# Per-partition scaling of attention probabilities as 64 instructions on ScalarE or VectorE, in a two-layer decoder kernel

## The chip, the cores and the metric

The kernel runs on one core of one Trainium2 chip. The metric is the device time of one execution in microseconds (us). Before the change the median of three runs is 612.57 us (611.25 to 612.8).

The engines are named as the profile names them: PE is TensorE (matmuls), PEld its weight load, DVE is VectorE, ACT is ScalarE, POOL is GpSimd, and SP is the queue that issues the loads of weights. Each engine works through its own queue in order and waits on semaphores for the others.

## The reference

Two layers over 256 positions of width 1024. Layer 0 mixes positions with a recurrent block, layer 1 with sparse attention; a squared-ReLU MLP of width 4096 follows each, and all sit between RMS norms. The change is in the attention of layer 1, 16 heads of width 64 in 4 groups of keys and values. It has three branches; with 256 positions, all of the 4 key blocks may be selected and the window of 512 holds everything, so two branches are dense causal attention over their own keys and values, and the third attends to 15 compressed keys:

```python
p = jnp.where(mask, jnp.exp(s - m), 0.0)
return p / jnp.maximum(jnp.sum(p, axis=-1, keepdims=True), 1e-30)
...
o = g[..., 0:1] * o_c + g[..., 1:2] * o_s + g[..., 2:3] * o_w
```

For each query row and each of the two dense branches the probabilities are thus divided by their sum and multiplied by a sigmoid gate: one factor per row and branch.

## The kernel before

Every fp32 product is made of three matmuls on halves: each operand is split into a rounded part (`hi`) and the rest (`lo`), and hi*hi, hi*lo and lo*hi are added (lines 305 to 307). So each weight piece of 128x1024 that is loaded costs a cast on ScalarE or VectorE (`whi`) and a subtraction on VectorE (`wlo`, line 310), beside its load on SP's queue. There are 5 buffers for raw weights and 7 for split ones.

The MLPs are loops written out by hand. The two mixers are sections whose order comes from a planner, `Plan`, that runs when the kernel is built. Each task is added with an engine (or a list of engines, each with a duration and a penalty), what it reads and writes, and a due time. `list_schedule` makes a first plan from the due times and a random shift drawn with a seed; six rounds of `forwards` and `backwards` replan it, each task going to the engine on which its end plus its penalty comes first; the plan that ends first sets the order in which instructions are emitted on each engine. Planner durations and due times set an order only; on the chip each engine waits for what it needs. The seed of the attention section is the second of `SEEDS`.

In the attention section, q, k and v are projected, and the 16 heads follow one another in the order of `heads`. Positions lie on 128 partitions in two query blocks: block 0 sees 128 keys and block 1 sees 256, for each of the two branches (`b`). So a head has four rows of probabilities, in the buffer `pt`: two of 128x128 and two of 128x256. The steps of a head, with the line numbers of the profile:
- `scores`: matmuls of q and k (1062, 1063); line 1069 on VectorE adds the positional term and the mask and leaves in `mx` the extreme of each row; line 1072 on ScalarE takes Exp with `mx` as its bias and accumulates the sum into `sm`.
- `rescale`: lines 1081, 1082 and 1084 on VectorE turn `sm` (128x4, one column per query block and branch) into the factors; line 1090 on VectorE multiplies `pt` by them, both branches of a query block in one instruction, so two instructions a head, of 128x256 and 128x512.
- `transposes`: line 1102 on TensorE turns the probabilities; line 1105 on ScalarE (`pth`) and line 1106 on VectorE (`ptl`) take them out of PSUM in two halves.
- `pv`: for each pair of heads, matmuls with the values (1121, 1132, 1134), then `osum` (1138 on ScalarE, 1141 on VectorE) and its split into `oh` and `ol`.

There are 3 buffers `pt`, 4 of `mx` and `sm`, and 4 transposed ones. Between the heads TensorE has other work of the section: projections of later q and k (809, 821 take them out of PSUM), and the first half of the output projection (487 adds it to `xt`). The second half follows behind the last head, and then the MLP of layer 1. Casts (`sa`, `sb`, `kh`, `oh`, line 313) may go to ScalarE or VectorE, as the planner finds.

Of the kernel before, what the change touches and what calls it, by code (L numbers as in the profile page):

```python
# [15 lines left out]
OP = mybir.AluOpType  # L16
# [3 lines left out]
P = 128  # L20
# [11 lines left out]
NPT, NTH = 3, 4  # L32
TSTAGE, FPS = 4.4, 3.0
CST = (0.5, 4.0, 8.5, 12.0)
SEEDS, ROUNDS, SHIFT = (11, 19), 6, 1.5
HPEN, LPEN, APEN, LEAD = 0.5, 1.0, 0.0, 9.0
WARM = 16
NI, NFINE = 3, 3
SQN = 2
# [37 lines left out]
class Plan:  # L77
# [8 lines left out]
    def add(self, eng, dur, fn=None, r=(), w=(), t=0.0, lag=None):  # L86

        if fn is None:
            eng, fn = eng, dur
        if isinstance(eng, str):  # L90
            eng = [(eng, dur, 0.0)]
        i, deps = len(self.tasks), set()
        for k in r:
            if k in self.writer:
                deps.add(self.writer[k])
            self.readers.setdefault(k, []).append(i)
        for k in w:
            deps.update(self.readers.pop(k, ()))
            if k in self.writer:
                deps.add(self.writer[k])  # L100
            self.writer[k] = i
        deps.discard(i)
        self.tasks.append((eng, fn, sorted(deps), t, lag))
# [113 lines left out]
def trunk_kernel(ctx: ExitStack, tc: tile.TileContext, x_in, vec_in, const_in, w2_in, wts, out):  # L217
    nc = tc.nc
    ctx.enter_context(tc.manual_schedule())
    pe, dve, act, pool = nc.tensor, nc.vector, nc.scalar, nc.gpsimd  # L220
# [9 lines left out]
    def bank(i):  # L230
        return psum.tile([P, 512], F32, name="bank%d" % i, tag="bank%d" % i)
# [258 lines left out]
    with ExitStack() as ph:  # L490
        rg = ph.enter_context(tc.tile_pool(name="rg", bufs=1))
        sec = Section()
        add, table = sec.add, sec.table
# [33 lines left out]
        wz = bank(7)[:, :S]  # L527
        for i in range(WARM):
            pe.matmul(wz, warm[:, :P], warm, start=True, stop=True)

        x2 = rg.tile([P, KC, S], F32, name="x2")
        for k in range(KC):
            g = vec[:, V_GM + k:V_GM + k + 1]
            t = 0.6 * k - 3
            add("act", 0.4, lambda e, k=k, g=g: e.activation(hh[:, k], xt[:, k], AF.Identity, scale=g),
                r=[("xt", k), "vec0"], w=[("hh", k)], t=t)
            add("dve", 0.4, lambda e, k=k, g=g: e.scalar_tensor_tensor(  # L537
                hl[:, k], xt[:, k], g, hh[:, k].bitcast(F32), op0=OP.mult, op1=OP.subtract), r=[("xt", k), "vec0"],
                w=[("hh", k)], t=t)
# [3 lines left out]
        for q in range(4):  # L543
            for i in range(NFINE):
                w = slice(256 * q, 256 * q + 256)
                hi, lo, rw = hi_t[i][:, w], lo_t[i][:, w], raw_t[i][:, w]
                rk = [("raw0", i, q), ("raw", i)]
                t = 1.2 * q + 0.3 * i - 2.9
                add([("dve", 0.2, 0.0), ("act", 0.31, 0.5)], copy(hi, rw), r=rk, w=[("hi0", i, q)], t=t)
                add("dve", 0.34, diff(lo, rw, hi), r=rk + [("hi0", i, q)], w=[("lo0", i, q)],  # L550
                    t=t + 0.1)
        for a, b, n in ((0, 2, 2), (0, 1, 1), (4, 6, 2), (4, 5, 1), (0, 4, 1)):
            add("dve", 0.07 + 0.267 * n, lambda e, a=a, b=b, n=n: e.tensor_tensor(
                x2[:, a:a + n], x2[:, a:a + n], x2[:, b:b + n], op=OP.add), r=[("x2", b + i) for i in range(n)],
                w=[("x2", a + i) for i in range(n)], t=4 + a / 4)
# [44 lines left out]
        def nextbank():  # L600
            zb["n"] += 1
            return (0, 1, 2, 3, 4, 5, 7)[(zb["n"] - 1) % 7]
# [102 lines left out]
        for m in range(8):  # L705
            wh, wl, wk = sec.weight("out", m, to + 2.65 * m)
            b = nextbank()
# [7 lines left out]
            t = to + 2.65 * (m + 1)  # L715
# [55 lines left out]
    with ExitStack() as ph:  # L771
        at = ph.enter_context(tc.tile_pool(name="at", bufs=1))
        sec = Section()
        add, weight, proj_t, zview, table = sec.add, sec.weight, sec.proj, sec.bank, sec.table
# [79 lines left out]
        for i in range(2):  # L854
            pecol = (V_PEK, V_PEV)[i]
            add("pool", 0.15, lambda e, i=i, c=pecol: e.tensor_copy(zfs[i][:, 60], vec[:, c:c + 16]), w=[("zf", i, "p")],
                t=-5)
# [218 lines left out]
        def rescale(s, t):  # L1076
            p, c, hf = heads[s]
            h = (2 * p + hf) * 4 + c
            sm, pt = sms[s % 4], pts[s % NPT]
            k2 = [("sm", s % 4, j) for j in range(4)]  # L1080
            add("dve", 0.07, lambda e: e.tensor_scalar(sm, sm, 1e-30, None, op0=OP.max), w=k2, t=t)
            add("dve", 0.09, lambda e: e.reciprocal(sm, sm), w=k2, t=t)
            s2_ = sm.rearrange("p (q b) -> p q b", q=2)
            add("dve", 0.07, lambda e: e.tensor_tensor(s2_, s2_, gts[:, :, h, 1:3], op=OP.mult),
                r=[("gt", 0), ("gt", 1)], w=k2, t=t)
            for qc in range(2):
                nk = (qc + 1) * P
                v = pt[:, qc * 2 * P:qc * 2 * P + 2 * nk].rearrange("p (b k) -> p b k", b=2)
                add("dve", (0.34, 0.6)[qc],
                    lambda e, v=v, qc=qc, nk=nk: e.tensor_tensor(  # L1090
                        v, v, sm[:, 2 * qc:2 * qc + 2, None].to_broadcast([P, 2, nk]), op=OP.mult),
                    r=[("sm", s % 4, 2 * qc + b) for b in range(2)], w=[("pt", s % NPT, qc, b) for b in range(2)], t=t + 0.2)

        def transposes(s, t):
            pt = pts[s % NPT]
# [51 lines left out]
        def out_t(half, m, b, t, step):  # L1147
            wh, wl, wk = weight("o%d" % half, m // 2, t)
            z = zview(("out", half, m), b, zcols)
            for ks in ((0, 1), (2, 3)) if half == 0 else ((0, 1), (2,), (3,)):  # L1150
                def run(e, ks=ks):
                    for kk in ks:
                        o = (m % 2) * 512 + kk * P
                        k = half * 4 + kk
                        mm3(z(), wh[:, o:o + P], wl[:, o:o + P], oh[k], ol[k], kk == 0, kk == 3)
                add("pe", 0.33 * len(ks), run, r=wk + [(n, half * 4 + kk) for n in ("oh", "ol") for kk in ks],
                    w=[("ps", b)], t=t)
                t += step * len(ks) / 2
            add("dve", 0.34, lambda e: residual(z(), m), r=[("ps", b)], w=[("xt", m)], t=t)
            return t  # L1160
# [29 lines left out]
        for i, (nm, c) in enumerate(fillers):  # L1190
            t = T0 + 4 * i * step
            b = i % 2
# [3 lines left out]
        for m in range(8):  # L1196
            t = T0 + (n0 + 2 * m) * step
            events.append((t, 0, lambda m=m, t=t: out_t(0, m, (len(fillers) + m) % 2, t, step)))
        for s in range(16):
            events.append((T0 + s * T, 1, lambda s=s: scores(s, T0 + s * T)))  # L1200
            events.append((T0 + (s + 1) * T - 1.5, 1, lambda s=s: rescale(s, T0 + (s + 1) * T - 1.5)))
            events.append((T0 + (s + 1.6) * T, 1, lambda s=s: transposes(s, T0 + (s + 1.6) * T)))
# [8 lines left out]
        for m in range(8):  # L1211
            t = out_t(1, m, (2, 3, 4, 0, 1)[m % 5], te - 2 + 1.4 * m, PJ)
# [131 lines left out]
```

## Time and profile before

| | before |
|---|---|
| median of three runs | 612.57 us |
| profiled execution, its time | 611.19 us |
| profiled execution, its span from first to last instruction | 609.1 us |
| PE busy | 580.3 us |
| DVE busy | 455.2 us |
| ACT busy | 362.2 us |
| mean granted TensorE clock | 0.981 |

The span is the time between the first and the last instruction; the time holds 2.1 us more that lie around it. Busy times are unions of the instructions' times. An instruction's duration overlaps with its neighbour's on the same engine by some 0.1 us where neither waits, so that a row of instructions costs less than the sum of their durations; the distance from start to start is then the cost of one.

### The profile page before, as it was taken

Reading aid. Unit: us, or ns where it says so; the run is one execution under the profiler, and the core shown is the slowest. Engines: PE = TensorE matmul, PEld = TensorE weight load, DVE = VectorE, ACT = ScalarE, POOL = GpSimd, SP = SyncE. Lnnn points to the kernel's source line nnn. Section 1 sums busy time; section 2 is a strip of 40 time slices with the busy share of each in tenths; the row PEclk is TensorE's granted clock in tenths of the full one; section 3 lists DMA queues with packets and bytes.
Section 4 is the critical chain, followed back from the end, with each engine's and each line's share of the span. In section 5 each row is a group of like instructions: output and inputs, shape, how many; then the busy total and the mean of one; then the engine's idle time right before and its main releaser. Section 6 shows DMA issues by size and latency. Waiting matters only on the chain.

```text
span 609.1 us, 12332 instructions
## 1 busy us (share of the span) xinstructions
PE 580.3 (95%) x4867; PEld 565.9 (93%) x4867; DVE 455.2 (75%) x929; ACT 362.2 (59%) x692; POOL 47.8 (8%) x57
## 2 busy tenths in 40 slices
PE   8979999999999999999999877899999999999994
PEld 7969999999999999999998766798999999999994
DVE  6999998767666556469989998999876677355432
ACT  7889775856564334256768866676675655343320
POOL 2210000000001122130010000000000000132220
PEclk9989999999999999999999998899999999999997
DMA  8755465656656655645640022125766666656401
GB/s 298 250 164 173 150 232 186 231 190 197 192 191 209 206 176 197 217 149 179 243 139 2 0 71 69 36 70 174 242 196 189 203 188 202 233 150 215 158 1 69
DMA packets 29178, 101.07 MB, mean 166 GB/s; under 512 B 3376, under 2 KB 4016, under 8 KB 29120
## 3 DMA queue, kind: packets, MB, share of 16 engines
q1 hardware_dynamic: 28512, 99.70, 49.8%
q8 instruction: 38, 0.62, 0.4%
q10 hardware_dynamic: 576, 0.53, 0.3%
q14 instruction: 20, 0.16, 0.1%
q0 software_dynamic: 32, 0.05, 0.0%
HBM read 99.22 MB, written 1.05 MB: 165 GB/s over the span
## 4 chain that ended last, share of the span: by engine, by line
PE 78%; DVE 16%; ACT 3%; issue 1%; DMA 1%; POOL 0%; SPq 0%; DVEq 0%; POOLq 0%; ACTq 0%
PE bank L306 24%; PE bank L305 24%; PE bank L307 24%; DVE wlo L310 2%; DVE ptl L1106 2%; DVE pt L1069 2%; DVE pt L1090 2%; DVE osum L1141 1%; DVE xb L624 1%; DMA raw<-in_dram 1%; PE bank L944 1%; PE bank L945 1%; PE bank L946 1%; ACT whi L313 1%; PE bank L1134 1%
## 5 line engine op out<-in xcount | busy, mean ns | idle before, releaser
L305 PE MATMUL bank<-hhl,whi 128*128 128x256 f32 x768 | 214.3, 279 | 2.4 <-DVE whi L313 1.4
L306 PE MATMUL bank<-hhl,whi 128*128 128x256 f32 x768 | 212.9, 277 | 0.1
L307 PE MATMUL bank<-hhl,wlo 128*128 128x256 f32 x768 | 212.7, 277 | 0.2 <-DVE wlo L310 0.2
L305 PEld LDWEIGHTS bank<-hhl,whi 128*128 128x128 f32 x768 | 144.5, 188 | 3.3 <-ACT x L541 1.6
L274 DVE TENSOR_TENSOR wlo<-raw,whi 128x1024 fp32r<-128x1024 f32 x115 | 143.6, 1269 | 2.3 <-ACT whi L265 2.3
L306 PEld LDWEIGHTS bank<-hhl,whi 128*128 128x128 f32 x768 | 144.5, 188 | 0.5 <-DVE hhl L537 0.3
L307 PEld LDWEIGHTS bank<-hhl,wlo 128*128 128x128 f32 x768 | 144.4, 188 | 0.4 <-DVE wlo L310 0.4
L305 PE MATMUL bank<-uhl,whi 128*128 128x256 f32 x512 | 141.5, 276 | 0.0
L306 PE MATMUL bank<-uhl,whi 128*128 128x256 f32 x512 | 141.4, 276 | 0.0
L307 PE MATMUL bank<-uhl,wlo 128*128 128x256 f32 x512 | 141.4, 276 | 0.0
L265 ACT CAST whi<-raw 128x1024 fp32r<-128x1024 f32 x116 | 118.0, 1039 | 23.0 <-issue 18.8
L305 PEld LDWEIGHTS bank<-uhl,whi 128*128 128x128 f32 x512 | 96.1, 188 | 0.0
L306 PEld LDWEIGHTS bank<-uhl,whi 128*128 128x128 f32 x512 | 96.1, 188 | 0.0
L307 PEld LDWEIGHTS bank<-uhl,wlo 128*128 128x128 f32 x512 | 96.1, 188 | 0.0
L310 DVE TENSOR_TENSOR wlo<-raw,whi 128x1024 fp32r<-128x1024 f32 (+2 forms) x80 | 86.1, 1099 | 1.6 <-ACT whi L313 1.4
L313 ACT CAST whi<-raw 128x1024 fp32r<-128x1024 f32 (+2 forms) x74 | 71.5, 978 | 13.8 <-DMA raw<-in_dram 8.4
L487 DVE TENSOR_TENSOR xt<-xt,bank 128x256 f32<-128x256 f32 x40 | 16.1, 413 | 84.5 <-PE bank L307 84.4
L736 ACT ACTIVATE u<-t 128x256 f32<-128x256 f32 x64 | 26.7, 417 | 57.6 <-DVE t L731 56.3
L731 DVE SCALAR_TENSOR_TENSOR t<-bank,rstd 128x256 f32<-128x256 f32 x64 | 26.9, 423 | 42.4 <-PE bank L307 42.2
L1072 ACT ACTIVATE pt<-pt,mx 128x128 f32<-128x128 f32 (+1 forms) x64 | 28.9, 451 | 7.5 <-DVE mx L1069 6.6
L1222 ACT ACTIVATE xg<-xt,vec 128x256 f32<-128x256 f32 x8 | 4.1, 511 | 47.9 <-DVE xt L487 47.9
L305 PE MATMUL bank<-xbh,whi 128*128 128x256 f32 x96 | 28.2, 294 | 4.2 <-ACT xbh L313 2.3
(207 smaller groups left out, 856.1 us busy)
## 6 DMA issues: line engine op xcount, KB each, us to landing
raw<-in_dram SPq DMA_DIRECT2D x179, 512.0 KB, 4.3
raw<-in_dram SPq DMA_DIRECT2D x4, 560.0 KB, 5.2
raw<-in_dram SPq DMA_DIRECT2D x6, 256.0 KB, 5.1
xt<-in_dram SPq DMA_DIRECT2D x4, 256.0 KB, 5.1
cst<-in_dram SPq DMA_DIRECT2D x1, 304.0 KB, 5.7
out_dram<-xg SPq DMA_DIRECT2D x2, 128.0 KB, 2.3
out_dram<-xg ACTq DMA_DIRECT2D x2, 128.0 KB, 2.4
out_dram<-xg SPq DMA_DIRECT2D x1, 256.0 KB, 2.3
```

Source lines behind the costliest of these rows:

```text
L265: (act.copy if eng is None else eng.tensor_copy)(hi_t[i % NSPL][:, :n], raw_t[i % NRAW][:, :n])
L274: (eng or dve).tensor_tensor(lo[:, :n], raw_t[i % NRAW][:, :n], hi[:, :n].bitcast(F32), op=OP.subtract)
L305: pe.matmul(ps, wh, xh, start=start, stop=False)
L306: pe.matmul(ps, wh, xl, start=False, stop=False)
L307: pe.matmul(ps, wl, xh, start=False, stop=stop)
L310: return lambda e: e.tensor_tensor(o, a, h.bitcast(F32), op=OP.subtract)
L313: return lambda e: (e.copy if e is act else e.tensor_copy)(o, a)
L487: dve.tensor_tensor(xt[:, m], xt[:, m], z, op=OP.add)
L731: dve.scalar_tensor_tensor(t, z, 0.0, rs, op0=OP.max, op1=OP.mult)
L736: act.activation(u, t, AF.Square)
L1069: add("dve", (0.2, 0.34)[qc], lambda e, sp_=sp_, b=b, qc=qc, nk=nk, row=row, j=j: e.tensor_tensor_reduce(row, sp_()[:, b], cst[:, C_D0 + q ...
L1072: add("act", (0.39, 0.49)[qc], lambda e, row=row, j=j: e.activation(row, row, AF.Exp, bias=mx[:, j:j + 1], scale=-1.0, accum_out=sm[:, j:j ...
```

## The change

The two multiplications of a head become four, one for each query block and branch. Each has a factor per partition as a scalar operand in place of a broadcast tensor. Each may go to ScalarE (`mul`) or to VectorE (`tensor_scalar`); the planner is given 0.2 and 0.31 us for ScalarE and 0.15 and 0.21 us for VectorE with a penalty of 1.0. The seed of the attention section is another.

```diff
-SEEDS, ROUNDS, SHIFT = (11, 19), 6, 1.5
+SEEDS, ROUNDS, SHIFT = (11, 3), 6, 1.5
 HPEN, LPEN, APEN, LEAD = 0.5, 1.0, 0.0, 9.0
+RPEN = 1.0
...
             for qc in range(2):
                 nk = (qc + 1) * P
-                v = pt[:, qc * 2 * P:qc * 2 * P + 2 * nk].rearrange("p (b k) -> p b k", b=2)
-                add("dve", (0.34, 0.6)[qc],
-                    lambda e, v=v, qc=qc, nk=nk: e.tensor_tensor(
-                        v, v, sm[:, 2 * qc:2 * qc + 2, None].to_broadcast([P, 2, nk]), op=OP.mult),
-                    r=[("sm", s % 4, 2 * qc + b) for b in range(2)], w=[("pt", s % NPT, qc, b) for b in range(2)], t=t + 0.2)
+                for b in range(2):
+                    j, o = 2 * qc + b, qc * 2 * P + b * nk
+                    add([("act", (0.2, 0.31)[qc], 0.0), ("dve", (0.15, 0.21)[qc], RPEN)],
+                        lambda e, v=pt[:, o:o + nk], c=sm[:, j:j + 1]: (
+                            e.mul(v, v, c) if e is act else e.tensor_scalar(v, v, c, None, op0=OP.mult)),
+                        r=[("sm", s % 4, j)], w=[("pt", s % NPT, qc, b)], t=t + 0.2)
```

The planner makes a new order of the whole attention section from this. Up to the end of layer 0's MLP the order on every engine is the one of before, and SP's order is the same throughout. In the kernel after, line numbers behind line 37 are one higher, and behind the change two or three.

The first place is VectorE at the fourth head of the section (its factors are `sm_3330`), early in the attention. Before:

```order
L1081 TENSOR_SCALAR sm_3330<-sm_3330 128x4
L1069 ISA pt,mx_3323<-bank_4101,cst 128x128
L1069 ISA mx_3323 128x1
L1082 RECIPROCAL sm_3330<-sm_3330 128x4
L1106 TENSOR_TENSOR ptl<-bank_4107,pth 128x384
L1084 TENSOR_TENSOR sm_3330<-sm_3330,gts 128x4
L1106 TENSOR_TENSOR ptl<-bank_4113,pth 128x384
L1090 TENSOR_TENSOR pt<-pt,sm_3330 128x256
L1090 TENSOR_TENSOR pt<-pt,sm_3330 128x512
L1141 TENSOR_TENSOR osum<-osum,bank_4082 64x256
```

The same head on VectorE in the change:

```order
L1082 TENSOR_SCALAR sm_3330<-sm_3330 128x4
L1108 TENSOR_TENSOR ptl<-bank_4127,pth 128x384
L1083 RECIPROCAL sm_3330<-sm_3330 128x4
L1143 TENSOR_TENSOR osum<-osum,bank_4100 64x256
L1108 TENSOR_TENSOR ptl<-bank_4120,pth 128x384
L1143 TENSOR_TENSOR osum<-osum,bank_4100 64x256
L1070 ISA pt,mx_3323<-bank_4132,cst 128x256
L1070 ISA mx_3323 128x1
L1070 ISA pt,mx_3323<-bank_4132,cst 128x256
L1070 ISA mx_3323 128x1
L1085 TENSOR_TENSOR sm_3330<-sm_3330,gts 128x4
```

And on ScalarE in the change, the four multiplications of that head between the Exps (line 1073) of the next:

```order
L1073 ACTIVATE pt,sm_3327<-pt,mx_3323 128x128 x2
L314 CAST sb_3295<-tt_3300 64x256
L314 CAST oh<-osum 128x256
L1073 ACTIVATE pt,sm_3327<-pt,mx_3323 128x256
L1093 ACTIVATE pt<-pt,sm_3330 128x128
L1093 ACTIVATE pt<-pt,sm_3330 128x256 x2
L1093 ACTIVATE pt<-pt,sm_3330 128x128
L1073 ACTIVATE pt,sm_3327<-pt,mx_3323 128x256
L1107 CAST pth<-bank_4195 128x384
L1107 CAST pth<-bank_4202 128x384
```

The factors are made in the same three steps on VectorE, and their use has gone to ScalarE's queue, ahead of one Exp of the next head and of two casts `pth`. So it is for 63 of the 64 instructions; one, of 128x256, is on VectorE.

The second place is the end of the section, the last head (again `sm_3330`). On VectorE before, with the second half of the output's `xt` and the weights of the MLP around it:

```order
L1081 TENSOR_SCALAR sm_3330<-sm_3330 128x4
L310 TENSOR_TENSOR wlo_96<-raw_81,whi_89 128x1024
L1082 RECIPROCAL sm_3330<-sm_3330 128x4
L487 TENSOR_TENSOR xt<-xt,bank_4886 128x256
L1084 TENSOR_TENSOR sm_3330<-sm_3330,gts 128x4
L487 TENSOR_TENSOR xt<-xt,bank_4924 128x256
L1106 TENSOR_TENSOR ptl<-bank_4957,pth 128x384
L1090 TENSOR_TENSOR pt<-pt,sm_3330 128x256
L1141 TENSOR_TENSOR osum<-osum,bank_4919 64x256
L1106 TENSOR_TENSOR ptl<-bank_4962,pth 128x384
L1141 TENSOR_TENSOR osum<-osum,bank_4919 64x256
L1090 TENSOR_TENSOR pt<-pt,sm_3330 128x512
```

On ScalarE in the change, from the multiplications of the last head to the table load:

```order
L1140 COPY osum<-bank_4951 64x256
L1093 ACTIVATE pt<-pt,sm_3330 128x256
L1093 ACTIVATE pt<-pt,sm_3330 128x128
L1093 ACTIVATE pt<-pt,sm_3330 128x256
L1093 ACTIVATE pt<-pt,sm_3330 128x128
L314 CAST whi_86<-raw_80 128x1024
L314 CAST oh<-osum 128x256
L1107 CAST pth<-bank_5033 128x384
L1107 CAST pth<-bank_5038 128x384
L314 CAST whi_87<-raw_81 128x1024
L314 CAST whi_88<-raw_82 128x1024
L1140 COPY osum<-bank_5063 64x256 x2
```

Before, the load of the table for the next function stood ahead of the last two `oh` casts on ScalarE; in the change it stands behind the last of them.

## The prediction

> **What bounds the kernel now.** I read the page's busy shares first. They name TensorE (PE), but they are a mean over stages with different limits.
>
> ```profile
> PE 580.3 (95%) x4867; PEld 565.9 (93%) x4867; DVE 455.2 (75%) x929; ACT 362.2 (59%) x692; POOL 47.8 (8%) x57
> ```
>
> Second, the chain of work that ended last, for the place of the change. In it the first row of the attention on VectorE (DVE) and the last row before TensorE takes over for good are these:
>
> ```profile
> 314.32 0.33 DVE pt L1069
> ...
> 417.73 0.35 DVE ol L310
> 418.12 0.39 PE bank L306
> ```
>
> Between them the chain is mostly VectorE's. Third, the busy times by stretch: one window ahead of the attention, five within it, two behind it. The columns are the window, its length, and the busy time of PE, its weight load, DVE, ACT and POOL.
>
> ```profile
> 270.00:314.00 44.00, 43.88 (x411) 43.28 (x410) 41.14 (x78) 29.15 (x48) 4.19 (x12) 1.00 0.56 185
> ...
> 314.00:335.00 21.00, 20.11 (x150) 18.05 (x149) 20.52 (x91) 18.28 (x58) 0.00 (x0) 1.00 0.06 24
> 335.00:360.00 25.00, 22.03 (x153) 18.56 (x151) 24.53 (x90) 18.66 (x55) 0.00 (x0) 1.00 0.07 22
> 360.00:380.00 20.00, 14.34 (x75) 12.24 (x75) 17.69 (x70) 12.63 (x42) 0.00 (x0) 0.83 0.22 68
> 380.00:405.00 25.00, 22.26 (x149) 20.18 (x150) 24.20 (x93) 17.48 (x53) 0.00 (x0) 0.93 0.16 52
> 405.00:418.00 13.00, 12.12 (x90) 10.82 (x89) 12.88 (x26) 8.61 (x17) 0.00 (x0) 1.00 0.42 134
> sum 104.00, PE 90.86 PEld 79.85 DVE 99.81 ACT 75.66 POOL 0.00; mean PE 18.17 PEld 15.97 DVE 19.96 ACT 15.13 POOL 0.00
> ...
> 418.00:440.00 22.00, 21.88 (x192) 21.88 (x193) 20.66 (x42) 14.98 (x31) 0.00 (x0) 1.00 0.66 221
> 440.00:609.00 169.00, 161.06 (x1417) 160.59 (x1415) 93.38 (x127) 76.70 (x122) 18.78 (x13) 0.98 0.52 164
> ```
>
> The sum row is the reading that matters. In the 104 us of the attention VectorE works 99.81 us, TensorE 90.86 and ScalarE (ACT) 75.66. VectorE is the bound here, and only here: ahead of 314 us and behind 418 us TensorE is full (43.88 of 44, 21.88 of 22). So a microsecond that this stretch loses moves everything behind it forward by a microsecond, and a new order ahead of 314 us changes nothing as long as TensorE stays fed. The waits of ScalarE inside the stretch say who follows whom:
>
> ```profile
> ACT pt L1072 <- DVE mx L1069: 6.6, 11, 1.1
> ACT osum L1138 <- PE bank L1132: 3.9, 5, 1.8
> ACT oh L313 <- DVE osum L1141: 3.2, 5, 1.4
> ...
> DVE osum L1141 <- ACT osum L1138: 1.5, 2, 1.1
> DVE pt L1069 <- PE bank L1063: 0.9, 1, 0.9
> ```
>
> ScalarE waits for VectorE; VectorE's own waits are 1.5 and 0.9 us and no more of that size. No row has VectorE waiting for a probability buffer.
>
> **What the change removes.** Sixteen heads had two multiplications each on VectorE:
>
> ```profile
> L1090 DVE TENSOR_TENSOR pt<-pt,sm 128x512 f32<-128x512 f32 x16 | 11.0, 684 | 0.1
> L1090 DVE TENSOR_TENSOR pt<-pt,sm 128x256 f32<-128x256 f32 x16 | 6.6, 414 | 0.0
> ...
> 322.01 1.02 DVE L1090 TENSOR_TENSOR pt<-pt,sm 128x512 f32<-128x512 f32 x2
> 322.95 0.19 DVE L1020 RECIPROCAL cm<-cm 128x8 f32<-128x8 f32 x1
> ```
>
> The durations overlap, so I price by the distance of starts: the pair began at 322.01 and the next instruction at 322.95, so a head gives back 0.94 us and sixteen heads 15.0 us of VectorE.
>
> **What it adds.** The order of the change puts 63 of the 64 new instructions on ScalarE and one on VectorE, so "or VectorE" is nearly empty. No row of before has this very multiplication, but two kinds of row are its like: ScalarE's activations that read a value per partition from memory, as Exp does with its bias and line 406 with its scale.
>
> ```profile
> 315.20 0.39 ACT L1072 ACTIVATE pt<-pt,mx 128x128 f32<-128x128 f32 x1
> 315.50 0.19 ACT L1072 ACTIVATION_READ_ACCUMULATOR pt<-pt,mx 128x1 f32 x1
> ...
> 420.69 0.40 ACT L410 ACTIVATE sq<-xt 128x256 f32<-128x256 f32 x1
> 421.00 0.49 ACT L406 ACTIVATE hhl<-xt,vec 128x256 fp32r<-128x256 f32 x1
> 421.39 0.40 ACT L410 ACTIVATE sq<-xt 128x256 f32<-128x256 f32 x1
> ```
>
> From start to start 128x128 takes 0.30 us (315.20 to 315.50) and 128x256 takes 0.39 (421.00 to 421.39), which I round to 0.40. A head has two of each: 1.40 us, and sixteen heads 22.4 us of ScalarE. The bounds of this price: below, an activation with no such operand. Line 410's starts are 0.31 us apart (420.69 to 421.00), and 0.10 less for half the row gives 1.04 us a head, which is also what the planner's table assumes (0.31 and 0.20). Above, no overlap at all, the whole durations:
>
> ```profile
> L1072 ACT ACTIVATE pt<-pt,mx 128x256 f32<-128x256 f32 x32 | 16.1, 505 | 3.9 <-DVE mx L1069 3.6
> L1072 ACT ACTIVATE pt<-pt,mx 128x128 f32<-128x128 f32 x32 | 12.7, 398 | 3.5 <-DVE mx L1069 3.0
> ```
>
> That is 1.81 us a head. I take 1.40, since the operand is there and the rows above are those of neighbours in one queue. So the planner made its order with ScalarE 0.36 us a head (5.8 us in all) cheaper than I expect it to be.
>
> The Trainium skill has a rule that speaks against this change: "ScalarE: Activation LUTs", section "Rules for kernel authors", says that multiplications belong on VectorE and not on ScalarE. Its reason there is bf16 work. For fp32 the page "VectorE: DVE Perf Modes", section "The perf-mode tier table", gives a tensor-scalar twice the rate of a tensor-tensor; from its 1227 ns for 2048 elements at two a cycle I estimate 0.29 and 0.22 us for the two sizes, 16.4 us of busy time for all 64, where the removed rows had 17.6. By that rule VectorE would gain about 1 us and ScalarE would get nothing; no run here shows it. The plan does the opposite, and what that would do at worst is the second rival.
>
> **What it moves.** The planner shifts work to make room. Between the first Exp and the last `oh` cast on ScalarE, the order has `whi` casts down from 12 to 11, `oh` from 6 to 4, `kh` from 6 to 4, `sb` from 5 to 4, and the table load has gone behind the last `oh`. At 0.31 us for a cast and about 1.0 for a `whi` this is 2.5 us off ScalarE. VectorE takes them at about 0.2 us each (0.6 for the `whi`) and one more `wlo` of 1.1 us: some 3 us back of the 15.
>
> ```profile
> L313 DVE CAST oh<-osum 128x256 fp32r<-128x256 f32 x2 | 0.5, 274 | 0.0
> L310 DVE TENSOR_TENSOR wlo<-raw,whi 128x1024 fp32r<-128x1024 f32 x12 | 14.5, 1213 | 0.0
> ```
>
> The table load (about 1.5 us with its dummy) now stands ahead of line 410, which waited for line 487 anyway; I put it at nothing, and at 1.5 us if `xt` comes earlier. SP's queue is the same row for row, so the loads are in the same order. Only memsets and small copies change places on POOL, 40 us ahead of the stretch, and I put them at nothing under TensorE's 43.88 busy of 44.
>
> **The sum.** The heads per stretch come from the removed line's own windows (two instructions a head):
>
> ```profile
> 314.00:335.00 21.00, 4.15 (x8) 1.00 0.06 24
> 335.00:360.00 25.00, 4.23 (x8) 1.00 0.07 22
> 360.00:380.00 20.00, 3.20 (x6) 0.83 0.22 68
> 380.00:405.00 25.00, 3.25 (x7) 0.93 0.16 52
> 405.00:418.00 13.00, 1.93 (x4) 1.00 0.42 134
> ```
>
> That is 4, 4, 3, 3 and 2 heads. Each stretch then lasts as long as its fullest engine, with DVE less 0.94 and ACT plus 1.40 a head:
> - 314 to 335: DVE 16.8, ACT 18.28 + 5.6 = 23.9, PE 20.1. ACT decides: 2.9 us longer.
> - 335 to 360: DVE 20.8, ACT 24.3, PE 22.0. ACT: 0.7 shorter.
> - 360 to 380: DVE 14.9, ACT 16.8, PE 14.3. ACT: 3.2 shorter.
> - 380 to 405: DVE 21.4, ACT 21.7, PE 22.3. PE: 2.7 shorter.
> - 405 to 418: DVE 11.0, ACT 11.4, PE 12.1. PE: 0.9 shorter.
>
> Together 4.6 us shorter. The 2.5 us that leave ScalarE fall in the first three, where ScalarE decides: 7.1 shorter. Against this stands that no engine is filled without gaps: in before the fullest one lost 4.2 of 104 us. Charged whole, that leaves 2.9 us; not charged, 7.1. ScalarE's busy time holds short tails that close up when its queue is full, and VectorE can run ahead now, so I take the middle: **5.1 us**. The profiled execution of 611.19 us would be 606.1; it lies 1.4 us under the median of the runs, 612.57, and from the median it is **607.5 us**.
>
> With ScalarE's price at its ends: at 1.04 us a head the first three stretches shrink by 4.0 us more and the gain is about 9; at 1.81 they grow by 4.5 and the fourth by 0.6, and nothing is left (about 612.6).
>
> **What is queued behind the new wait.** A multiplication on ScalarE waits for line 1084's `sm` on VectorE. Behind it in ScalarE's queue stand the next head's Exps and the `pth` casts, for which TensorE's next matmuls and VectorE's `ptl` wait. So a late `sm` now holds up ScalarE too, where before it held up VectorE alone.
>
> **Rivals.**
> 1. VectorE stays the bound and everything comes back: 15.0 less the 3 us of moved work, 12 us, 600.6. For it: VectorE fills 99.81 of 104 today. Against it: ScalarE would have to do 75.66 + 22.4 - 2.5 = 95.6 us of busy time in 92.
> 2. The other side: ScalarE becomes a serial bound. Place: the first 45 us, where it is busy 18.28 of 21 and 18.66 of 25. Today it idles 28 of the 104 us, in waits for `mx`, for `o` and for `osum`. With 95.6 us of work it may idle only 8.4 us before the stretch is longer than it was. If half of today's idle time stays, 14 us, the stretch is 109.6 us and the time 618.2. The point at which it is measurably slower is 10.2 us of idle time. For it: the planner priced ScalarE 5.8 us too low, and its queue is in order. Against it: most of those waits are for VectorE, which gets lighter. The skill's rule named above would lead here.
> 3. No difference that can be told: the first stretch grows by 2.9, and the gaps eat what the later ones give, since three engines with 91 to 96 us of work must fit into about 100. Time 612. For it: TensorE's 22.0 of 25 and 12.1 of 13 leave little room. Against it: its clock of 0.83 in 360 to 380 us comes with its idle time there, which would shrink.
> 4. The change doing nothing because the planner leaves the work on VectorE is excluded by the order: 63 of 64 went to ScalarE.
>
> **How the numbers follow.** Forecast (3 to 9 us shorter) 0.58, rival 1 0.12, rival 2 0.16, rival 3 0.14. Within 0.3% (1.8 us, about what can be told here) is rival 3; so faster 0.70, same 0.14, slower 0.16. The forecast's own range is 603.5 to 610. The range of 8 in 10 reaches below to half of rival 1, 602, and above over rival 3 and the price's upper bound, 613.5; left out are rival 2 and the far part of rival 1.
>
> **What would show it.** In the changed profile: a row for line 1091 or so on ScalarE, x63, with means near 505 and 398 ns (right) or 410 and 300 (price too high); VectorE's busy time in the attention near 88 us; ScalarE near 95 us with under 6 us of idle time; the change from attention to TensorE's full stretch at about 413 us in place of 418. Wrong would be ScalarE rows for the multiplication with long idle time before them put down to `sm`, VectorE waiting for `pt` from ScalarE or TensorE, or a first stretch that is over 24 us long.

## The result, and the profile after

The changed kernel takes **601.37 us** (median of four runs, 601.02 to 602.11) where the one before takes 612.52 in the same session (611.25 to 612.8). The ratio is 0.9824, with a 95% interval of 0.9806 to 0.9841: 11.1 us faster. The forecast was 607.5 us, with a range of 602.0 to 613.5. The direction was right; the gain is more than twice the 5.1 us forecast, and the time lies just below the range. Two single executions further down, one of 967 us (the kernel before with seed 3) and one of 2022 us (no operand per partition), ran in a far slower state than the others and are left out of the ratios.

Where it went shows in one window per kernel, from the first row of line 1069 (1070 after) on VectorE to the end of the last `ol`, with the stretch behind it to the end of the span. The columns are the window, its length, and the busy time of PE, its weight load, DVE, ACT and POOL; then the granted clock and the transfers. Before:

```profile
314.20:418.10 103.90, 90.66 (x610) 79.65 (x608) 99.74 (x366) 75.49 (x221) 0.00 (x0) 0.95 0.16 53
...
418.10:609.10 191.00, 182.94 (x1606) 182.47 (x1606) 113.94 (x168) 91.67 (x151) 18.78 (x13) 0.98 0.53 171
```

After:

```profile
313.70:408.20 94.50, 85.98 (x606) 74.46 (x604) 89.88 (x343) 89.75 (x276) 0.00 (x0) 1.00 0.20 64
408.20:599.30 191.10, 183.00 (x1606) 182.53 (x1606) 113.10 (x168) 92.41 (x153) 18.80 (x13) 0.99 0.52 168
```

Nearly all of it is in the attention. The profiled span is 9.8 us shorter (609.1 to 599.3): the attention went from 103.9 us to 94.5, it began 0.5 us earlier, and the stretch behind it is 191.0 and 191.1 us. (The rest of the 11.1 us is in the choice of execution: the profiled one of the kernel before took 1.3 us less than the median, that of the change 0.3 less.) VectorE went from 99.74 to 89.88 us of work, ScalarE from 75.49 to 89.75: the two are equal to within 0.2 us now. The fuller of the two is idle for 4.6 us in the attention; before it was 4.2. TensorE's clock, 0.95 in the attention before, is 1.00.

ScalarE's waits inside the attention, the longest five:

```profile
ACT whi L314 <- PE bank L307: 1.4, 1, 1.4
ACT pt L1093 <- DVE sm L1085: 1.3, 4, 0.4
ACT oh L314 <- DVE osum L1143: 0.9, 1, 0.9
ACT pt L1073 <- DVE mx L1070: 0.7, 2, 0.5
ACT sa L314 <- DVE tt L810: 0.4, 2, 0.3
```

Exp waited 6.6 us in total for `mx`; now 0.7. The wait of ScalarE that the change adds, for `sm`, is 1.3 us in four pieces. Of the 28.4 us that ScalarE idled in the attention, 4.75 are left. TensorE also waits more for the multiplications than before: its weight loads for the transposes waited 1.4 us in total for those on VectorE, and now wait 6.0 us for those on ScalarE.

```profile
PEld bank L1104 <- ACT pt L1093: 6.0, 14, 1.0
```

TensorE is not the fullest engine of the attention (85.98 us of 94.5), and the attention is shorter in spite of these waits.

### The profile page after: what moved, and what is told of

Same layout as the page of the kernel before. It is cut to its first block, busy times and chain, and to the rows that moved or that the text cites. A ratio compares the mean times of both kernels' runs of the same rounds, so it can differ in the third digit from the quotient of the medians.

```text
span 599.3 us, 12366 instructions
## 1 busy us (share of the span) xinstructions
PE 575.3 (96%) x4867; PEld 560.1 (93%) x4867; DVE 444.1 (74%) x902; ACT 378.5 (63%) x751; POOL 47.6 (8%) x57
## 4 chain that ended last, share of the span: by engine, by line
PE 72%; DVE 13%; ACT 11%; DMA 2%; issue 2%; POOL 0%; SPq 0%; DVEq 0%; ACTq 0%; POOLq 0%
PE bank L307 23%; PE bank L308 23%; PE bank L306 23%; DVE wlo L311 3%; ACT pt L1073 3%; ACT pt L1093 3%; ACT whi L314 1%; DVE xb L625 1%; ACT pth L1107 1%; DMA xt<-in_dram 1%; DVE ptl L1108 1%; PE bank L945 1%; DMA raw<-in_dram 1%; DVE osum L1143 1%; PE bank L946 1%
## 5 line engine op out<-in xcount | busy, mean ns | idle before, releaser
L266 ACT CAST whi<-raw 128x1024 fp32r<-128x1024 f32 x116 | 118.0, 1039 | 22.9 <-issue 18.8
L314 ACT CAST whi<-raw 128x1024 fp32r<-128x1024 f32 (+2 forms) x73 | 70.0, 977 | 13.4 <-DMA raw<-in_dram 6.0
L458 POOL TENSOR_TENSOR acc<-xt 128x256 f32<-128x256 f32 x2 | 3.0, 1524 | 360.7 <-DVE xt L488 360.7
```

The costliest lines, as they stand in the source:

```text
L266: (act.copy if eng is None else eng.tensor_copy)(hi_t[i % NSPL][:, :n], raw_t[i % NRAW][:, :n])
L314: return lambda e: (e.copy if e is act else e.tensor_copy)(o, a)
```

## The experiments

The attention's length and the two loads, each run from its first row on VectorE to the end of its last `ol`, are the thread through all runs:

| kernel | time, us | attention, us | VectorE busy | ScalarE busy |
|---|---|---|---|---|
| before | 612.52 | 103.9 | 99.74 | 75.49 |
| the change | 601.37 | 94.5 | 89.88 | 89.75 |
| before, seed 3 | 612.22 | 103.1 | 101.39 | 73.50 |
| ScalarE in the old order | 620.66 | 113.6 | 86.91 | 95.50 |
| multiplications left out, old order | 606.71 | 99.3 | 86.75 | 74.74 |
| the change's order, on VectorE | 613.93 | 107.7 | 103.94 | 71.61 |
| planned anew, all on VectorE | 612.96 | 103.4 | 98.69 | 75.40 |
| half moved | 603.93 | 96.3 | 93.30 | 84.73 |
| no operand per partition | 599.27 | 92.1 | 89.31 | 84.89 |
| more work on ScalarE | 613.81 | 105.5 | 91.04 | 99.53 |
| ScalarE or GpSimd, seed 3 | 598.32 | 90.6 | 88.15 | 81.22 |

Behind the attention the span goes on for 191.0 to 192.9 us in each of these kernels. The times are medians; the three other columns are of one profiled execution, whose time lies up to 1.6 us from the median. Each ratio below is to the kernel before in the same session. Its median there was 611.53 to 611.80 us, some 0.8 us less than in the session of the result, so times of different sessions can be compared to about 1 us. The seed is 3 unless another is given; the kernels in the old order keep the seed 19 of the kernel before.

### Is it the seed?

The kernel before with the seed of the change:

```diff
-SEEDS, ROUNDS, SHIFT = (11, 19), 6, 1.5
+SEEDS, ROUNDS, SHIFT = (11, 3), 6, 1.5
```

> The kernel before, with seed 3 in place of 19 for the attention section; the two tensor-tensor multiplications a head stay on VectorE. Theory A (the load did it: 15 us left the engine that was full, and the new plan fills ScalarE's idle time; the seed is worth 2 us at most): 611 to 615 us, VectorE busy about 99 us between its first row of line 1069 and its last ol. Theory B (a luckier order: the seed gave a good part of the 11 us): 604 to 608.

Measured: 612.22 us, ratio 1.001 (0.9995 to 1.0026). And the changed kernel with the seed of before, and with two more (7 and 23):

```diff
-SEEDS, ROUNDS, SHIFT = (11, 3), 6, 1.5
+SEEDS, ROUNDS, SHIFT = (11, 19), 6, 1.5
```

> The changed kernel with seed 19 in place of 3. All 64 multiplications are on ScalarE by its order. Theory A (load): 600 to 604 us. Theory B (a lucky seed): 605 to 609.

> The changed kernel with seed 7. Theory E (each seed is a draw; 601.4 was a good one and 606.3 an ordinary one): 603 to 608 us. If seed 19 was an unlucky one and seed 3 ordinary: 600 to 603.

> The changed kernel with seed 23, for the spread of the draws. Theory E: 603 to 608 us. If seed 3 is ordinary: 600 to 603.

Measured: 606.31 us with seed 19, 604.95 with seed 7, 602.92 with seed 23 (ratios 0.9908, 0.9889, 0.9851). The four seeds of the change lie between 601.4 and 606.3, with a mean of 603.9; the two of before lie 0.6 us apart by their ratio. So the gain is 5 us or more with each of these seeds and some 8 us in their mean; 2.5 to 3 us of the 11.1 belong to a good draw. Theory A had allowed 2 us at most for the seed; some 5 us lie between 3 and 19, and the run with seed 19 fell into the range of theory B. The kernel before was drawn with two seeds only.

For seed 19 the place can be shown. Its profiled span is 6.0 us longer than the change's. Its attention is no longer (94.6 us from 315.0 to 409.6), but begins 1.3 us later; the rest of the loss comes in the norm behind it. Windows of that run, and TensorE's longest wait there:

```profile
420.00:425.00 5.00, 3.52 (x33) 3.43 (x31) 4.97 (x8) 3.79 (x5) 0.00 (x0) 1.00 0.65 192
425.00:430.00 5.00, 4.15 (x23) 4.16 (x24) 3.76 (x8) 2.58 (x8) 0.00 (x0) 0.69 0.95 340
430.00:435.00 5.00, 5.00 (x44) 5.00 (x44) 1.40 (x4) 2.58 (x5) 0.00 (x0) 0.97 0.25 101
...
PE bank L485 <- DVE rcol L399: 2.3, 1, 2.3
```

TensorE waits 2.3 us for the norm's `rcol`, until 425.85, and the clock it is granted from 425 to 430 is 0.69. The stretch behind the attention is 195.7 us there in place of 191.1: TensorE is idle 2.3 us longer in it, and busy 2.3 us longer (185.28 us in place of 183.00) with the same matmuls. In the change there is no such wait and the clock there is 1.00.

### The move without the new plan

The kernel before with its own plan, order and seed; only the instruction differs:

```diff
-                    lambda e, v=v, qc=qc, nk=nk: e.tensor_tensor(
-                        v, v, sm[:, 2 * qc:2 * qc + 2, None].to_broadcast([P, 2, nk]), op=OP.mult),
+                    lambda e, v=v, qc=qc, nk=nk: [
+                        act.mul(v[:, b], v[:, b], sm[:, 2 * qc + b:2 * qc + b + 1]) for b in range(2)],
```

> The kernel before with its own plan, seed and due times; only the instruction differs: where the plan has the multiplication on VectorE (0.34 or 0.6 us), two activations on ScalarE are emitted at that place. Nothing is planned anew. Theory A (load plus a new plan that fills ScalarE's idle time): without the new plan ScalarE's queue is ordered for other work, and the busy part of its waits stays: a part of the gain, 604 to 609 us. Theory C (the move alone does it, the plan hardly matters): 600 to 603. If ScalarE's order without room for it turns it into a serial bound (the second rival of the prediction): over 613.

Measured: **620.66 us**, ratio 1.0142 (1.012 to 1.0164): slower. Its attention and VectorE's longest waits in it:

```profile
314.50:428.10 113.60, 92.90 (x609) 81.15 (x608) 86.91 (x334) 95.50 (x285) 0.00 (x0) 0.94 0.15 47
...
DVE osum L1141 <- ACT osum L1138: 4.4, 5, 1.6
DVE ol L310 <- ACT oh L313: 4.2, 3, 1.9
DVE ptl L1106 <- ACT pth L1105: 3.4, 4, 1.2
DVE pc L1041 <- ACT pc L1040: 3.1, 3, 1.9
DVE pt L1069 <- PE bank L1063: 3.0, 2, 2.0
```

VectorE has 13 us less to do and takes 9.7 us longer, because it now waits for ScalarE at `osum`, `oh`, `pth` and `pc`: 15.1 us in these four rows, where the kernel before had 1.5 for `osum` and no other of that size. ScalarE's queue has the multiplications at places where the old order had left it no time for them. This is the mechanism of the prediction's second rival, which put the time at 618.2, and theory A's 604 to 609 is missed. That the busy time of ScalarE agrees with the rival's (95.6 us, measured 95.50) is luck: the 95.6 count 2.5 us of casts that leave ScalarE, and in the old order none leave; without that term the working gives 98.1.

The same order with the multiplications left out:

```diff
-                    lambda e, v=v, qc=qc, nk=nk: e.tensor_tensor(
-                        v, v, sm[:, 2 * qc:2 * qc + 2, None].to_broadcast([P, 2, nk]), op=OP.mult),
+                    lambda e: None,
```

> The kernel before, its order kept, with the two multiplications of each head left out (the probabilities are not divided by their sums or gated; the factors are still made). It takes 15.0 us off VectorE and gives ScalarE nothing. Theory A (VectorE's load is the bound; a fixed order lets TensorE and ScalarE take part of it back): 600 to 605 us. If the order of before holds its length by other engines: 606 to 611.

Measured: 606.71 us (ratio 0.9914, 0.9897 to 0.9931).

```profile
314.10:413.40 99.30, 87.69 (x610) 79.20 (x608) 86.75 (x334) 74.74 (x221) 0.00 (x0) 0.95 0.18 55
```

Of the 13 us that leave VectorE's busy time, 4.6 leave the attention. So an order made for a full VectorE gives back a third of what is taken from it, even when nothing is put elsewhere. Theory A had asked for 600 to 605; the time is in the other range, in which the order holds its length by other engines.

### The new plan without the move

The change's plan and order, with a tensor-scalar on VectorE at every place where the plan has ScalarE:

```diff
-                            e.mul(v, v, c) if e is act else e.tensor_scalar(v, v, c, None, op0=OP.mult)),
+                            dve.tensor_scalar(v, v, c, None, op0=OP.mult)),
```

> The changed kernel's plan and order, seed 3, but at each place where the plan has a multiplication on ScalarE a tensor-scalar on VectorE is emitted (it took 0.92 us a head there). Theory A (plan and load belong together: the plan alone gives nothing): VectorE has its 15 us back in a queue with no room for it, 612 to 620 us. Theory C2 (the plan is better by itself): 604 to 609.

Measured: 613.93 us (ratio 1.0031, 1.0017 to 1.0044). VectorE is full again and ScalarE idles:

```profile
313.90:421.60 107.70, 90.10 (x606) 76.89 (x604) 103.94 (x406) 71.61 (x213) 0.00 (x0) 0.97 0.18 56
...
ACT pt L1073 <- DVE mx L1070: 11.6, 15, 1.8
ACT pth L1107 <- PE bank L1104: 8.3, 8, 2.4
```

The plan alone is worth nothing, and the move alone costs 9 us. Together they are worth 11. This plan counts on a lighter VectorE and has moved casts to it, so it is a hard test of a plan with the multiplications on VectorE; but plans made with them there from the start gain nothing either (612.22 us for the kernel before with seed 3, and 612.96 in the next run).

### The form of the instruction

VectorE as the only engine offered, planned anew:

```diff
-                    add([("act", (0.2, 0.31)[qc], 0.0), ("dve", (0.15, 0.21)[qc], RPEN)],
+                    add([("dve", (0.15, 0.21)[qc], 0.0)],
```

> The change with VectorE as the only engine offered: 64 tensor-scalar instructions on VectorE, seed 3, planned anew at the planner's 0.15 and 0.21 us. Theory A (load): ScalarE gets nothing, VectorE loses only what the single-source form saves. By the cast rows of 128x256 on VectorE (0.20 us from start to start, about 0.13 for half) that is 0.66 in place of 0.94 us a head, 4.5 us in all: 607 to 609 us. Theory D (the gain is the new form of instruction, not the engine): 601 to 603. An estimate from the Trainium skill, VectorE: DVE Perf Modes, section The perf-mode tier table, gives about 1 us: 611.

Measured: 612.96 us, ratio 1.002 (1.0005 to 1.0035). The new form saves VectorE nothing:

```profile
L1093 DVE TENSOR_SCALAR pt<-pt,sm 128x256 f32<-128x256 f32 x32 | 10.4, 346 | 0.0
L1093 DVE TENSOR_SCALAR pt<-pt,sm 128x128 f32<-128x128 f32 x32 | 8.4, 279 | 0.0
```

These are 18.8 us of busy time in place of 17.6. I had priced it by the cast of 128x256, 274 ns; with a factor per partition it takes 346. The Trainium skill ("VectorE: DVE Perf Modes", section "The perf-mode tier table") led to an estimate of 290 and 220 ns and of about 1 us of gain; the measured rows are 56 to 59 ns longer, and the gain is nil. Theory A's 607 to 609 is missed.

### Which engine is the limit now

The change's order with a constant in place of the factor per partition (left out: the division by the sums and the gates):

```diff
-                            e.mul(v, v, c) if e is act else e.tensor_scalar(v, v, c, None, op0=OP.mult)),
+                            e.mul(v, v, 0.25) if e is act else e.tensor_scalar(v, v, c, None, op0=OP.mult)),
```

> The changed kernel with its order kept; ScalarE's 63 multiplications take the constant 0.25 in place of the factor per partition, so the probabilities are not divided by their sums or gated (that part of the computation is left out, its factors are still made). It takes 0.09 us off each, 5.8 us off ScalarE, and its waits for sm. Theory A with ScalarE as the fullest engine: 596 to 599 us. If VectorE's load (89.9 of 94.5 us) decides alone: 600.5 to 602.

And the change's order with 32 more activations on ScalarE:

```diff
-                            e.mul(v, v, c) if e is act else e.tensor_scalar(v, v, c, None, op0=OP.mult)),
+                            [e.mul(v, v, c)] + [e.mul(v, v, 1.0) for _ in range(int(v.shape[1] == P))] if e is act else
+                            e.tensor_scalar(v, v, c, None, op0=OP.mult)),
```

> The changed kernel, its order kept; after each of the 32 multiplications of 128x128 ScalarE multiplies the same row once more by the constant 1.0: 32 times 0.21 us, 6.7 us more on ScalarE and nothing elsewhere. If ScalarE is a full bound: all of it, 607 to 608 us. If VectorE and ScalarE share the bound, as the run without the operand suggests (2.1 us for 5.8): 603 to 606. If ScalarE has room: 601 to 602.

Measured: 599.27 us and 613.81. Their windows:

```profile
313.80:405.90 92.10, 84.36 (x606) 74.45 (x604) 89.31 (x343) 84.89 (x276) 0.00 (x0) 1.00 0.21 65
```

```profile
313.80:419.30 105.50, 88.81 (x606) 77.06 (x604) 91.04 (x343) 99.53 (x308) 0.00 (x0) 0.97 0.19 57
```

Taking 4.9 us off ScalarE's busy time shortens the attention by 2.4; adding 9.8 lengthens it by 11.0. So the two are not alike: downwards VectorE, with 89.3 us, is next in line; upwards ScalarE is the bound and the attention grows by all that is added and a little more. The first time lies between its two expectations, so neither engine decides alone; a constant needs no `sm`, so the 1.3 us of waits for it are gone as well, and not all of the 2.4 us need come from the busy time. None of the expectations had over 608 for the second run: the added rows take 0.31 us each where I had 0.21. TensorE's clock in its attention is 0.97.

The planner's price of ScalarE at the measured values, seed 3:

```diff
-                    add([("act", (0.2, 0.31)[qc], 0.0), ("dve", (0.15, 0.21)[qc], RPEN)],
+                    add([("act", (0.3, 0.4)[qc], 0.0), ("dve", (0.15, 0.21)[qc], RPEN)],
```

> The changed kernel, seed 3, planned with ScalarE's measured pitch (0.3 and 0.4 us in place of 0.2 and 0.31). Theory A (the load and ScalarE's filled queue make the time; the planner's wrong price costs a little): 599 to 603 us, at best 1 to 2 us under the change. Theory E (the price is irrelevant to the time; every replan is a new draw of the order, worth several us either way): 602 to 607.

Measured: 605.80 us (ratio 0.9906, 0.9886 to 0.9926), no better than the draws of the other seeds. Its VectorE has more to do, since the planner moved casts there to make room on ScalarE:

```profile
314.30:413.00 98.70, 88.38 (x605) 78.66 (x604) 93.06 (x351) 88.75 (x269) 0.00 (x0) 0.95 0.20 61
```

In this one draw, then, the wrong price did no harm: with it the planner had left those casts on ScalarE. Theory A's 599 to 603 is missed, and the time is as theory E has it. Moving half (the first query block stays on VectorE as a tensor-tensor, the second goes to ScalarE):

```diff
+                if qc == 0:
+                    v = pt[:, :2 * nk].rearrange("p (b k) -> p b k", b=2)
+                    add("dve", 0.34, lambda e, v=v, nk=nk: e.tensor_tensor(
+                        v, v, sm[:, 0:2, None].to_broadcast([P, 2, nk]), op=OP.mult),
...
+                    continue
```

> The change for the second query block alone, seed 3, planned anew: 32 multiplications of 128x256 on ScalarE, and the 16 tensor-tensor ones of 128x256 of the first query block on VectorE as before. VectorE loses 9.6 us of 15.0, ScalarE gains 12.5 of 22. Theory A (the time goes with the fullest engine, VectorE at about 93 to 95 us, and some 4.5 us of gaps): 604 to 607 us. If ScalarE's load was the limit of the full move: under 601.

Measured: 603.93 us (ratio 0.9884, 0.9859 to 0.9908).

```profile
314.90:411.20 96.30, 85.34 (x606) 74.45 (x604) 93.30 (x357) 84.73 (x247) 0.00 (x0) 1.00 0.20 62
```

VectorE's load is 93.30 and the attention 96.3, so the time again follows the fuller of the two engines.

### A third engine

GpSimd is idle in the attention. Offered at guessed prices, and then at prices near those measured:

```diff
-                    add([("act", (0.2, 0.31)[qc], 0.0), ("dve", (0.15, 0.21)[qc], RPEN)],
+                    add([("act", (0.2, 0.31)[qc], 0.0), ("dve", (0.15, 0.21)[qc], RPEN), ("pool", (0.5, 0.8)[qc], 0.0)],
```

> The change with GpSimd offered as a third engine for the multiplications, at 0.5 and 0.8 us (guesses; GpSimd's rows of other forms are 1.2 to 1.5 us for 128x256 with two inputs). By its order 31 are on ScalarE and 33 on GpSimd, which is idle in this stretch. If a row takes about 0.8 us or less there: ScalarE is 11 us lighter and the time 596 to 600. If it takes 1.4 us or more, or slows VectorE down: over 603.

Measured: 602.72 us, between the two ranges and no better than the change. Its rows on GpSimd:

```profile
L1093 POOL TENSOR_SCALAR pt<-pt,sm 128x256 f32<-128x256 f32 x15 | 15.3, 1023 | 27.4 <-DVE sm L1085 24.9 <-PE bank L1104 2.5
L1093 POOL TENSOR_SCALAR pt<-pt,sm 128x128 f32<-128x128 f32 x18 | 12.6, 705 | 35.3 <-DVE sm L1085 22.5 <-ACT pt L1073 4.9 <-DVE cm L1020 4.2
```

With 0.72 and 1.04 us for GpSimd and the measured prices for the others (seed 13 and no penalty on VectorE in the first of these runs, whose line is shown; seeds 19 and 3 and the penalty of 1.0 in the other two):

```diff
-                    add([("act", (0.2, 0.31)[qc], 0.0), ("dve", (0.15, 0.21)[qc], RPEN)],
+                    add([("act", (0.3, 0.4)[qc], 0.0), ("dve", (0.21, 0.25)[qc], RPEN), ("pool", (0.72, 1.04)[qc], 0.0)],
```

> The three engines at measured prices and no penalty: ScalarE 0.3 and 0.4 us, VectorE 0.21 and 0.25, GpSimd 0.72 and 1.04; seed 13. By its order 22 multiplications are on ScalarE, 10 on VectorE, 32 on GpSimd. If the loads of VectorE and ScalarE are the limit: ScalarE about 13 us lighter, VectorE 2 heavier, 597 to 602 us. If handing work between engines is the limit by now: 602 to 606.

> As the run with three engines, with the penalty of 1.0 us kept on VectorE; seed 19. By its order 29 multiplications are on ScalarE and 35 on GpSimd. If the loads are the limit: 596 to 601 us, ScalarE about 78 us busy. If VectorE, about 90 us, decides alone: 601 to 603.

> The same with seed 3; 28 on ScalarE, 36 on GpSimd. The same expectations, and within 3 us of the run with seed 19 if the seeds differ no more than those of the change did without their clock dips.

Measured: 600.99, 601.16 and **598.32 us**. The last has a ratio of 0.9776 (0.9758 to 0.9793) to the kernel before, whose interval lies wholly below the change's: a version that beats both kernels. It is the best of four draws with GpSimd; but at these prices both runs with a seed that the change was run with are ahead of it (598.32 to 601.37 with seed 3, 601.16 to 606.31 with seed 19). These plans also have ScalarE's measured price, which by itself gave 605.80 with seed 3. The attention of the fastest:

```profile
313.90:404.50 90.60, 83.18 (x606) 74.27 (x604) 88.15 (x340) 81.22 (x244) 27.11 (x35) 1.00 0.22 66
...
DVE ol L311 <- ACT oh L314: 0.2, 1, 0.2
DVE pt L1070 <- PE bank L1064: 0.2, 1, 0.2
```

ScalarE is 8.5 us lighter than in the change, and VectorE, with 88.15 of 90.6 us and hardly a wait, is the only full engine again. The seed 19 has the same 90.6 us of attention (314.4 to 405.0); in the profiled execution, the fastest of its four, it begins 0.5 us later and loses 1.0 us behind it (193.0 us in place of 192.0).

## Why the prediction was right and wrong

**VectorE is the bound, only here, and what the attention loses comes off the end.** Right: 191.0 us behind the attention before, 191.1 after, and between 191.0 and 193.0 in all other runs but one (seed 19 of the change, 195.7). Both kernels that put the multiplications back on VectorE are within 2.2 us of before. That VectorE is the bound holds for an order that is made anew: with the old order kept, 13.0 us less work on it took 4.6 us off the attention.

**15.0 us leave VectorE, 3 come back.** Right in kind, and the first figure too large: with the multiplications left out of the old order 13.0 us leave VectorE's busy time (99.74 to 86.75), and in the change 9.9 (99.74 to 89.88), where I had 12. So some 3 us came back, as forecast.

**The price on ScalarE.** Right as the distance of starts in a row:

```profile
L1093 ACT ACTIVATE pt<-pt,sm 128x256 f32<-128x256 f32 x31 | 15.0, 501 | 0.3 <-DVE sm L1085 0.3
L1093 ACT ACTIVATE pt<-pt,sm 128x128 f32<-128x128 f32 x32 | 12.2, 393 | 0.9 <-DVE sm L1085 0.9
...
383.78 1.49 ACT L1093 ACTIVATE pt<-pt,sm 128x256 f32<-128x256 f32 x4 [0.34 <-DVE sm L1085]
385.17 0.29 ACT L1017 ACTIVATE cs<-cs 128x128 f32<-128x128 f32 x1
```

A head's four took 1.39 us from start to start; I had 1.40. As what they add to ScalarE's busy time it was too high, as follows.

**ScalarE's busy time** is the step that failed. The prediction put it at 75.66 + 22.4 - 2.5 = 95.6 us, which made ScalarE the fullest engine and the one that decides the first three stretches; 89.75 were measured. The run with the change's order on VectorE takes the two terms apart. ScalarE has 71.61 us there without the multiplications, so the new order moves 3.9 us off it (75.49 to 71.61), where I had 2.5; and the multiplications add 18.1 us (71.61 to 89.75), where I had 22.4. In the old order they add 20.0 (75.49 to 95.50). The 63 durations of 501 and 393 ns sum to 28.1 us, so each overlaps by 0.16 us, where my price had 0.10. That this comes from gaps that the multiplications fill, so that the tails of the instructions ahead of them are covered too, is argued and not shown.

**The sum, stretch by stretch.** Its stretches came to 96.9 us for the fullest engine, and 2.0 us of gaps made 98.9 us of attention. Measured are 89.9 and 4.6, together 94.5. So the load was 7.0 us too large, 5.9 of it by ScalarE's busy time, and the gaps were 2.6 us too small. With the measured terms (1.13 us a head, 3.9 us moved out of the first three) the same five stretches sum to 92.5, and with the 2.0 us of gaps to 94.5. That it meets the measured length to the tenth is luck, since the gaps were larger, but it shows that the size of ScalarE's term failed, more than the division into stretches. A sum of this kind holds only where the order is made for the loads: in the old order the attention took 113.6 us with no engine busy for more than 95.5.

I also took each of the five windows as a box whose work stays in it. The plan does not keep the boxes; taking it so added 1.3 us (96.9 where ScalarE's load alone was 95.6). Windows of the change's line 1093 on VectorE and ScalarE, and of all engines, over the first three boxes:

```profile
314.00:335.00 21.00, 0.34 (x1) 5.55 (x15) 1.00 0.15 49
335.00:360.00 25.00, 0.00 (x0) 6.29 (x16) 1.00 0.06 22
360.00:380.00 20.00, 0.00 (x0) 6.60 (x16) 1.00 0.24 80
```

```profile
314.00:335.00 21.00, 19.97 (x145) 17.50 (x144) 19.80 (x86) 20.33 (x69) 0.00 (x0) 1.00 0.15 49
335.00:360.00 25.00, 21.68 (x153) 18.60 (x152) 23.36 (x92) 23.51 (x76) 0.00 (x0) 1.00 0.06 22
360.00:380.00 20.00, 17.41 (x114) 14.16 (x113) 19.20 (x78) 19.42 (x59) 0.00 (x0) 1.00 0.24 80
```

The first 21 us hold as many heads' multiplications as before, four, with ScalarE busy for 20.33 us where I had 23.9. The third holds four heads where it held three.

**The gaps.** 4.2 us of 104 for the fullest engine before, 4.6 of 94.5 after: charged whole this term would have been nearly right, and I charged half. By itself that would have made the forecast worse (2.9 us of gain): it hid a part of the error in the load. (The middle of 2.9 and 7.1 is 5.0, and not 5.1.)

**Rival 1, VectorE stays the bound**, at 0.12, came nearest in time: 600.6. The case against it rested on ScalarE's 95.6 us in 92, the figure that failed. Its mechanism was half right: the attention lost 9.4 us where VectorE lost 9.9, but VectorE did not stay the bound alone, as the run without the operand shows.

**Rival 2, ScalarE as a serial bound.** It did not happen in the change, and it did in the two runs that give ScalarE work for which the order has no room: 620.66 and 613.81 us. Of the signs of being wrong that the prediction names, ScalarE's waits for `sm` are 1.3 us, and VectorE has no wait for `pt`.

The rule of the Trainium skill ("ScalarE: Activation LUTs", section "Rules for kernel authors") that multiplications belong on VectorE would have cost some 12 us here: VectorE alone takes 612.96 us planned anew with the same seed. For the single instruction the traces agree with the rule: 346 and 279 ns on VectorE, 501 and 393 on ScalarE. Here it is the load of the fuller engine that counts.

**Rival 3, no difference**, fell with ScalarE's load. TensorE's clock did recover, from 0.95 to 1.00, but that is not the cause of the gain: the kernel before with seed 3 has a clock of 1.00 in its attention too, and is no faster:

```profile
314.00:417.10 103.10, 87.19 (x611) 75.30 (x610) 101.39 (x371) 73.50 (x217) 0.00 (x0) 1.00 0.19 57
```

Nor does the clock follow TensorE's idle time in the attention as a whole, as the rival had it: here it is 15.9 us at a clock of 1.00, and in the kernel before 13.2 us at 0.95.

**What stays open:** why seed 3 packs the change better than 7 or 23 (94.5 us of attention against 96.4 and 96.3, at loads within 0.8 us). Both have a lower clock, 0.98 in their attention; whether that is a cause was not tried.

## What to carry to other kernels

Where a planner orders the work, price a move by each engine's load over the whole region that is planned anew, and by the whole of the gaps that the fullest engine has there now; windows describe the old order only. Check the load that is added against a run in the new order: 18.1 us came onto ScalarE here (20.0 in the old order), where the distance of starts gave 22.4. Moving work from a full engine to one that was three quarters busy paid until the two were level, but only with a new order: the same move in the old order cost 9 us here, and the new order without the move gained nothing. When two engines are level, look for a third that idles, even at twice the price an instruction: planned at measured prices that was worth 3 to 5 us here, at guessed ones nothing.

## What the runs showed of the hardware that I had not expected

- A multiplication by a value per partition on VectorE takes 346 and 279 ns for 128x256 and 128x128 in fp32, no less than half of the tensor-tensor of the double size (684 and 414): splitting it there saves nothing.
- GpSimd takes 705 and 1023 ns for the same two, some two times ScalarE's 393 and 501. In the run with three engines five rows of each are on VectorE, all while GpSimd was busy, and have means of 336 and 397 ns in place of 279 and 346.
- In the change with seed 19 a wait of 2.3 us by TensorE was followed by a granted clock of 0.69 (425 to 430 us), and the stretch behind the attention was 4.6 us longer in all.
